# Moving the query, key and value loads of an attention core from GpSimd's DMA queue to SyncE's

## The chip, the cores and the metric

The kernel runs on one core of a Trainium2 chip. The metric is the time of one execution on the device in microseconds (us), the median over runs. The core has a tensor engine (PE, with its weight loads shown apart as PEld), VectorE (DVE), ScalarE (ACT), GpSimd (POOL) and SyncE (SP). SP computes nothing: it issues transfers (DMAs) on a queue of its own, in order, and each waits there for the buffers and data that it needs. GpSimd issues transfers too, between its own arithmetic, on a second queue. The profile calls the first queue q1, "hardware_dynamic", and GpSimd's q0, "software_dynamic". Both move their bytes with the same 16 DMA engines of the core.

## What is computed

The reference is a two-layer encoder trunk on 1024 tokens of 1024 features, all in float32: a retention layer, a squared-ReLU MLP, an attention layer, a second MLP and a last norm. The change touches the attention layer only. Cut to what matters:

```
q, k, v = split(h @ w_in, 3)              # 16 heads of 64 features
for each chunk c of 64 queries:           # 16 chunks
    keys  = the chunk itself and the 8 chunks before it
    s = q k^T * 64**-0.5 + bias[head][clipped distance]
    p = softmax(s);  o = p v
return o @ w_out
```

## The kernel before

Every float32 product is made from split operands: `hi` is the value rounded to the tensor engine's float32r, `lo` the rest, so a dense product is three matmuls (L162 to L164).

**Before the core.** `qk_proj(p)` (L712 to L733) computes queries and keys of a pair of heads with 96 such matmuls, splits them (`dhi` at L727, `t` at L729) and stores hi and lo in DRAM, in `qA[p]` and `kA[p]` (L733, eight stores for queries and eight for keys, on SP's queue). The buffers of `dhi` hold one tile for each half of the tokens, so the next split waits until the last one is stored. Values go to `vA` (L756). The order of work is p = 0 to 3, the values, then p = 4 to 7. The loads of heads 0 and 1 (L785 to L788) stand ahead of the last `qk_proj`, but each may run as soon as its data are in DRAM.

**The core.** It walks over 16 heads of four units each (`units`, L900). A unit is two blocks of 128 queries: `scores` (two products with the hi and the lo of the keys, L846 and L847; bias and minimum at L851; exponential at L855; scaling on GpSimd at L857), `turn` (transposes, L875, and a split) and `values` (L887, then sums and a split whose `lo` is GpSimd's, L141). Between them `fill.step` issues one group of the output product of earlier heads (`att_out`, from L162 to L164, `h` at L280), whose weights (`wraw`) come on SP's queue.

**The loads of a head** are asked for one head ahead, a step in each unit (`load_head`, L809 to L823):

- `load_q`: `qh`, 128 rows of 4 KB (64 hi rows and 64 lo rows). Two buffers.
- `load_k`: `kk`, 128 rows of 8 KB: 64 rows that hold keys' hi and lo, written twice, once for each half of the partitions. The source's pattern is `[[0, 2], [2 * S, DH], [1, 2 * S]]`: an outer step of two copies, then 64 rows, then 2048 words. 1 MB in all. Two buffers.
- `load_b`: `bt`, the bias, two transfers on SP's queue, and two small fills by GpSimd (L781, L782). Two buffers.
- the values: `vst`, 1024 pieces of 512 bytes. Three buffers.

A framework traces the program, lays every engine's instructions out in an order of its own that keeps the data's dependencies, and sets the waits. With two buffers, the keys of head n can be loaded once the last product of head n-2 that reads its keys (L847) is done.

Of the kernel before, what the change touches and what calls it, by code (L numbers as in the profile page):

```python
# [9 lines left out]
F32 = mybir.dt.float32  # L10
# [3 lines left out]
PSUM = bass.MemoryType.PSUM  # L14
DRAM = bass.MemoryType.DRAM

P = 128
# [9 lines left out]
DH = 64  # L27
# [15 lines left out]
def _tables():  # L43
    """Position tables: they depend on the shapes alone."""
    import numpy as np

    half = DK // 2
    inv = np.exp(-np.float32(np.log(10000.0)) * np.arange(half, dtype=np.float32) / np.float32(half))
    ang = (np.arange(S, dtype=np.float32)[:, None] * inv.astype(np.float32)[None, :]).astype(np.float64)
    cos = np.cos(ang).T.astype(np.float32)  # L50
    sin = np.sin(ang).T.astype(np.float32)
    lg = _log_gamma()
    jp = np.arange(S) % HT
    vdec = np.exp(-lg[None, :] * (jp[:, None] + 1.0)) * RET_SCALE
    vdec = vdec.reshape(NB, P, RH).transpose(1, 0, 2)
    ip = np.arange(HT)
    odec = np.exp(lg[None, :] * (ip[:, None] + 1.0)).reshape(HT // P, P, RH).transpose(1, 0, 2)
    j = np.arange(P)[:, None]
    i = np.arange(P)[None, :]
    same = (j // CHUNK) == (i // CHUNK)  # L60
    mask = np.zeros((P, RH, P))
    for h in range(RH):
        m = np.where(i >= j, 1.0, 0.0)
        mask[:, h, :] = np.where(same & (i < j), np.exp(2.0 * lg[h] * (j - i)), m)
    f = lambda a: np.ascontiguousarray(a, dtype=np.float32)
    return {
        "cos": f(cos),
        "sin": f(sin),
        "vdec": f(vdec),
        "odec": f(odec),  # L70
        "odec2": f(odec * odec),
        "mask": f(mask),
    }
# [3 lines left out]
def trunk_kernel(ctx: ExitStack, tc: tile.TileContext, I, out):  # L77
# [34 lines left out]
    def load_gains(psp, pl, parts, g0):  # L112
        """Gains of 128 features in a row each, turned so that the features lie on the partitions."""
        n = sum(src.shape[0] for src in parts)
        rows = pl.tile([n, P], F32, name="grows", tag=f"grows{g0}")
        r = 0
        for src in parts:
            DMA.dma_start(out=rows[r:r + src.shape[0], :], in_=src)
            r += src.shape[0]

        def turn():
            pg = psp.tile([P, n], F32, name="pg", tag="ps")
            nc.tensor.transpose(pg, rows, ident[0:n, 0:n])
            nc.vector.tensor_copy(out=gall[:, g0:g0 + n], in_=pg)
        return turn
# [8 lines left out]
    def split(src, hi, lo, hi_eng="act", lo_eng="dve"):  # L134
        """hi: src rounded to the tensor engine's float32r; lo: what is left of src, exactly."""
        if hi_eng == "act":
            nc.scalar.copy(out=hi, in_=src)  # L137
        else:
            nc.vector.tensor_copy(out=hi, in_=src)
        eng = nc.vector if lo_eng == "dve" else nc.gpsimd  # L140
        eng.tensor_tensor(out=lo, in0=src, in1=hi.bitcast(F32), op=ALU.subtract)  # L141

    def wload(src, kb, cols):
        """Fetch one weight unit [128, kb, cols] (1024 columns)."""
        raw = wp.tile([P, kb, cols], F32, name="wraw", tag="wraw", bufs=2)
        DMA.dma_start(out=raw, in_=src.rearrange("(k p) c -> p k c", p=P))
        return raw
# [11 lines left out]
    def mm3(ps, lhs, rhs, start, stop):  # L159
        """Three products that carry a float32 product of split operands."""  # L160
        (lh, ll), (rh, rl) = lhs, rhs
        nc.tensor.matmul(ps, lhsT=lh, rhs=rh, start=start, stop=False)  # L162
        nc.tensor.matmul(ps, lhsT=lh, rhs=rl, start=False, stop=False)  # L163
        nc.tensor.matmul(ps, lhsT=ll, rhs=rh, start=False, stop=stop)  # L164
# [4 lines left out]
    def rsqrt_newton(sd, v, y):  # L169
        """y = v ** -0.5, one Newton step past the square root's table."""  # L170
        nc.scalar.activation(sd, v, AF.Sqrt)
        nc.vector.reciprocal(out=y, in_=sd)
        nc.vector.scalar_tensor_tensor(out=sd, in0=v, scalar=-0.5, in1=y, op0=ALU.mult, op1=ALU.mult)
        nc.vector.tensor_tensor(out=sd, in0=sd, in1=y, op=ALU.mult)
        nc.vector.scalar_tensor_tensor(out=y, in0=sd, scalar=1.5, in1=y, op0=ALU.add, op1=ALU.mult)

# [1 line left out]
    class Norm:  # L178
# [28 lines left out]
        def finish(self, psp, hf, col=False, row=True):  # L207
            """r = rsqrt(mean + eps) of a half: along the free axis in rB, along the partitions in rcol."""
            ah = self.gp.tile([P, HT], F32R, name="ah", tag="ah")
# [18 lines left out]
    def up_group(psp, norm, w, hf):  # L228
        """128 output features of one half of the tokens."""
        hi, lo = w  # L230
        ps = psp.tile([P, HT], F32, name="ps", tag="ps")
        for kb in range(NB):
            mm3(ps, (hi[:, kb, :], lo[:, kb, :]), (norm.hi[kb][hf], norm.lo[kb][hf]), kb == 0, kb == NB - 1)
        return ps
# [5 lines left out]
    def proj_tok(psp, norm, src, evac):  # L240
        """512 output features, tokens on the partitions: one bank for each block of tokens."""
        pss = [psp.tile([P, HT], F32, name="ps", tag="ps") for _ in range(NB)]
# [10 lines left out]
    def down(box, src, nk, rhs, hi_eng="act", lo_eng="dve"):  # L253
        """h += W^T rhs for nk blocks of features, one group at a step. box holds the PSUM pool and, where
        the blocks are final, their norm; blocks that were final before the norm was there follow."""
        cols = 1024 // nk
# [35 lines left out]
    class Filler:  # L292
        """Steps of a product that are issued between other work."""

# [42 lines left out]

    # ================= retention =================
    vS = [dram.tile([S, DV], F32, name=f"vS{i}") for i in range(RH)]
# [137 lines left out]
    with ExitStack() as ph:  # L477
# [6 lines left out]
        with ExitStack() as st:  # L484
# [5 lines left out]

            # Loads run in the order of use, a ring of raw tiles ahead of the splits.
            items = [(hd, hf, what) for hd in range(RH) for hf in range(2) for what in ("q", "k", "v0", "v1")]
# [33 lines left out]
            def turn_k(hd):  # L526
                """Keys of the first half with the tokens on the partitions."""
                kt[hd] = th, tl = [cp.tile([P, 4, DK], F32R, name=n, tag=n, bufs=1) for n in ("kth", "ktl")]
# [45 lines left out]
            def outs(hd, hf, pr):  # L574
                """Retention of two blocks of queries and their normalised rows."""
                pss, mv = [], cp.tile([P, 2, 2], F32, name="mv", tag="mv", bufs=2)
# [115 lines left out]

    # ================= first MLP =================
    with ExitStack() as ph:
# [3 lines left out]

    # ================= chunked attention =================
    w_in = I["att_w_in"][0]  # L700
# [6 lines left out]
    with ExitStack() as ph:  # L707
# [57 lines left out]
        def load_q(hd):  # L765
            T[hd, "q"] = cq.tile([P, S], F32R, name="qh", tag="qh", bufs=2)
            nc.gpsimd.dma_start(out=T[hd, "q"], in_=qA[hd // 2][hd % 2].rearrange("z f c -> (z f) c"))

        def load_k(hd):
            t = cq.tile([P, 2, S], F32R, name="kk", tag="kk", bufs=2)  # L770
            src = kA[hd // 2][hd % 2]
            nc.gpsimd.dma_start(out=t.rearrange("p z s -> p (z s)"), in_=bass.AP(tensor=src.tensor, offset=src.offset, ap=[[0, 2], [2 * S, DH], [1, 2 * S]]))
            T[hd, "k"] = [t[:, 0, :], t[:, 1, :]]
# [18 lines left out]
    with ExitStack() as ph:  # L792
# [7 lines left out]
        with ExitStack() as st:  # L800
# [8 lines left out]
            def load_head(hd, step):  # L809
                """Stacks that give all four partial products of q k in two passes, values and bias."""  # L810
                if step == 0:
# [8 lines left out]
                else:  # L820
                    t = cp.tile([P, NB, P], F32R, name="vst", tag="vst", bufs=3)
                    nc.gpsimd.dma_start(out=t, in_=vA[hd // 8][:, (hd % 8) * P:(hd % 8 + 1) * P].rearrange("(t p) c -> p t c", p=P))
                    T[hd, "v"] = t  # L823
# [11 lines left out]
            def scores(hd, g, z):  # L835
                """Probabilities of one block of queries; scores and bias come negated."""
                Q = 2 * g + z
# [97 lines left out]

    # ================= second MLP and the last norm =================
    with ExitStack() as ph:
        psp = pool(ph, "psF", None, 8, PSUM)
        with ExitStack() as st:
# [4 lines left out]
            def last(src, rhs):  # L944
                """The last part of the product, half by half: one half leaves while the other is computed."""
                ws = []
# [63 lines left out]
```

## Time and profile before

| | us |
|---|---|
| median of 3 runs | 3043.75 (3042.92 to 3044.22) |
| span of the profiled execution, first to last instruction | 3039.2 |
| PE busy in the span | 2871.2 (94%) |
| DVE, ACT, POOL busy | 1319.7, 880.3, 432.5 |
| GpSimd's queue q0: packets, MB, share of 16 engines | 35584, 33.61, 5.1% |
| SP's queue q1 | 220896, 207.19, 22.4% |

The profiled execution's own time lies outside the profile; its span is 4.55 us under the median of the runs. Busy times of one engine can be read as shares of the span; the idle time that matters is that of PE, and nearly all of it lies in two places of the attention layer.

### The profile page before, as it was taken

The page shows a single profiled execution, that of the slowest core. Times are in us where ns is not written, and L with a number is a line of the kernel's source. Part 1 is how long each engine was busy: PE and PEld are TensorE (multiplying, and loading weights), DVE is VectorE, ACT ScalarE, POOL GpSimd, SP SyncE. Part 2 cuts the span into 40 slices and gives each one's busy share as a digit, 9 for nine tenths or more (in the row PEclk, how much of TensorE's full clock was granted, in tenths as well). Part 3 has the DMA queues.
Part 4 walks back from the last instruction along what each step waited for, and adds up shares of the span by engine and source line. Part 5 has one row for each costly group of instructions (what it writes and reads, how often), then busy time and mean ns, then how long its engine had stood idle before and what let it go on. Part 6 is the DMA issues. An engine that isn't in the chain of part 4 may idle for free.

```text
span 3039.2 us, 33109 instructions
## 1 busy us (share of the span) xinstructions
PE 2871.2 (94%) x13178; PEld 2376.4 (78%) x13178; DVE 1319.7 (43%) x2194; ACT 880.3 (29%) x1484; POOL 432.5 (14%) x439
## 2 busy tenths in 40 slices
PE   8999999899999999999999899576879999999998
PEld 7888888677778888888888788465767888888887
DVE  6331133555565333333346233465668333333335
ACT  4012222432342221112223122564655111222213
POOL 4320000322230000000002000454533000000002
PEclk9999999899999999999999999788989999999999
DMA  4323333432111111111114546645521111111111
GB/s 138 106 87 103 108 105 96 158 104 90 63 49 43 48 49 49 49 49 49 49 46 133 149 147 162 120 95 115 113 68 42 49 49 49 49 46 45 49 49 70
DMA packets 258122, 245.86 MB, mean 81 GB/s; under 512 B 25048, under 2 KB 209440, under 8 KB 255920
## 3 DMA queue, kind: packets, MB, share of 16 engines
q1 hardware_dynamic: 220896, 207.19, 22.4%
q0 software_dynamic: 35584, 33.61, 5.1%
q10 hardware_dynamic: 1488, 2.95, 0.3%
q8 instruction: 103, 1.69, 0.2%
q14 instruction: 51, 0.42, 0.0%
HBM read 189.09 MB, written 57.19 MB: 81 GB/s over the span
## 4 chain that ended last, share of the span: by engine, by line
PE 83%; DMA 10%; DVE 4%; POOL 1%; ACT 1%; issue 1%; SPq 0%; POOLq 0%; ACTq 0%; DVEq 0%
PE ps L162 26%; PE ps L163 26%; PE ps L164 26%; DMA kk<-kA 7%; PE po L887 1%; PE pt L875 1%; DVE hlo L190 0%; DMA kA<-dhi 0%; PE pS L846 0%; POOL acc L200 0%; DMA xt<-in_x_dram 0%; PE pS L847 0%; PE pt L629 0%; DMA wraw<-in_att_w_in_dram 0%; DMA qA<-dhi 0%
## 5 line engine op out<-in xcount | busy, mean ns | idle before, releaser
L162 PE MATMUL ps<-hhi,whi 128*128 128x512 f32 x1792 | 699.3, 390 | 12.5 <-ACT whi L137 9.3
L163 PE MATMUL ps<-hlo,whi 128*128 128x512 f32 x1792 | 698.8, 390 | 1.4 <-DVE hlo L190 1.4
L164 PE MATMUL ps<-hhi,wlo 128*128 128x512 f32 x1792 | 698.5, 390 | 1.0 <-DVE wlo L141 0.9
L137 ACT CAST whi<-wraw 128x1024 fp32r<-128x1024 f32 x220 | 231.6, 1053 | 1255.1 <-PE ps L163 1023.4
L280 DVE TENSOR_TENSOR h<-ps,h 128x512 f32<-128x512 f32 x368 | 253.6, 689 | 467.5 <-PE ps L164 465.4
L162 PEld LDWEIGHTS ps<-hhi,whi 128*128 128x128 f32 x1792 | 337.2, 188 | 83.6 <-ACT whi L137 10.0
L163 PEld LDWEIGHTS ps<-hlo,whi 128*128 128x128 f32 x1792 | 337.3, 188 | 72.1 <-DVE hlo L190 2.1
L164 PEld LDWEIGHTS ps<-hhi,wlo 128*128 128x128 f32 x1792 | 337.1, 188 | 72.2 <-DVE wlo L141 2.1
L162 PE MATMUL ps<-uh,whi 128*128 128x512 f32 x960 | 379.7, 396 | 0.0
L163 PE MATMUL ps<-ul,whi 128*128 128x512 f32 x960 | 379.7, 396 | 0.0
L164 PE MATMUL ps<-uh,wlo 128*128 128x512 f32 x960 | 379.7, 396 | 0.0
L141 DVE TENSOR_TENSOR wlo<-wraw,whi 128x1024 fp32r<-128x1024 f32 x213 | 266.7, 1252 | 239.4 <-ACT whi L137 239.3
L200 POOL TENSOR_TENSOR acc<-acc,sq 128x512 f32<-128x512 f32 x70 | 102.4, 1465 | 1418.0 <-ACT sq L199 1412.2
L324 DVE SCALAR_TENSOR_TENSOR t<-ps,rB 128x512 f32<-128x512 f32 x128 | 88.0, 691 | 320.6 <-PE ps L164 320.6
L162 PEld LDWEIGHTS ps<-uh,whi 128*128 128x128 f32 x960 | 180.3, 188 | 43.7
L164 PEld LDWEIGHTS ps<-uh,wlo 128*128 128x128 f32 x960 | 180.3, 188 | 43.6
L163 PEld LDWEIGHTS ps<-ul,whi 128*128 128x128 f32 x960 | 180.3, 188 | 43.6
L846 PE MATMUL pS<-kk,qh 128*128 128x320 f32 (+1 forms) x192 | 70.0, 370 | 107.2 <-DMA kk<-kA 102.4
L325 ACT ACTIVATE t<-t 128x512 f32<-128x512 f32 x128 | 80.5, 630 | 262.1 <-DVE t L324 262.1
L162 PE MATMUL ps<-whi,hhi 128*128 128x512 f32 x384 | 149.4, 389 | 0.3 <-DVE vt L755 0.3
L164 PE MATMUL ps<-whi,hlo 128*128 128x512 f32 x384 | 149.4, 389 | 0.0
L163 PE MATMUL ps<-wlo,hhi 128*128 128x512 f32 x384 | 149.4, 389 | 0.0
(188 smaller groups left out, 3760.3 us busy)
## 6 DMA issues: line engine op xcount, KB each, us to landing
wraw<-in_mlp_w_dram SPq DMA_DIRECT2D x128, 512.0 KB, 3.7
wraw<-in_ret_w_in_dram SPq DMA_DIRECT2D x48, 512.0 KB, 4.0
kk<-kA POOLq DMA_DIRECT2D x16, 1024.0 KB, 27.4
wraw<-in_att_w_in_dram SPq DMA_DIRECT2D x24, 512.0 KB, 3.9
vS<-t SPq DMA_DIRECT2D x32, 256.0 KB, 2.0
gS<-t SPq DMA_DIRECT2D x32, 256.0 KB, 2.1
wraw<-in_ret_w_out_dram SPq DMA_DIRECT2D x16, 512.0 KB, 3.5
raw<-vS SPq DMA_DIRECT2D x16, 512.0 KB, 4.5
```

The costliest lines, as they stand in the source:

```text
L137: nc.scalar.copy(out=hi, in_=src)
L141: eng.tensor_tensor(out=lo, in0=src, in1=hi.bitcast(F32), op=ALU.subtract)
L162: nc.tensor.matmul(ps, lhsT=lh, rhs=rh, start=start, stop=False)
L163: nc.tensor.matmul(ps, lhsT=lh, rhs=rl, start=False, stop=False)
L164: nc.tensor.matmul(ps, lhsT=ll, rhs=rh, start=False, stop=stop)
L200: nc.gpsimd.tensor_tensor(out=self.acc[hf], in0=self.acc[hf], in1=sq, op=ALU.add)
L280: nc.vector.tensor_tensor(out=hv, in0=ps, in1=hv, op=ALU.add)
L324: nc.vector.scalar_tensor_tensor(out=t, in0=res[hf], scalar=0.0, in1=rB[:, hf * HT:(hf + 1) * HT], op0=ALU.max, op1=ALU.mult)
L325: nc.scalar.activation(t, t, AF.Square)
L846: nc.tensor.matmul(ps[:, y, :hw], lhsT=qs, rhs=kh[:, ks], start=True, stop=False)
L875: nc.tensor.transpose(pt[:, c - done:c - done + P], pr[:, (kb - k0) * P:(kb - k0 + 1) * P], ident)
L887: nc.tensor.matmul(po[:, oc:oc + n], lhsT=T[hd, "v"][:, kb, :], rhs=t[:, off[kb]:off[kb] + n], start=i == 0, stop=i == len(seq) - 1)
```

## The change

The three loads of a head go to SP's queue (`DMA` is `nc.sync`), and their destinations are named as float32 in place of float32r, so that source and destination have one type. Source patterns, destinations, sizes and buffers stay as they are. The diff also empties docstrings and comment lines, which issue nothing and keep the line numbers.

```diff
         def load_q(hd):
             T[hd, "q"] = cq.tile([P, S], F32R, name="qh", tag="qh", bufs=2)
-            nc.gpsimd.dma_start(out=T[hd, "q"], in_=qA[hd // 2][hd % 2].rearrange("z f c -> (z f) c"))
+            DMA.dma_start(out=T[hd, "q"].bitcast(F32), in_=qA[hd // 2][hd % 2].rearrange("z f c -> (z f) c"))
 
         def load_k(hd):
             t = cq.tile([P, 2, S], F32R, name="kk", tag="kk", bufs=2)
             src = kA[hd // 2][hd % 2]
-            nc.gpsimd.dma_start(out=t.rearrange("p z s -> p (z s)"), in_=bass.AP(tensor=src.tensor, offset=src.offset, ap=[[0, 2], [2 * S, DH], [1, 2 * S]]))
+            DMA.dma_start(out=t.rearrange("p z s -> p (z s)").bitcast(F32), in_=bass.AP(tensor=src.tensor, offset=src.offset, ap=[[0, 2], [2 * S, DH], [1, 2 * S]]))
             T[hd, "k"] = [t[:, 0, :], t[:, 1, :]]
...
                     t = cp.tile([P, NB, P], F32R, name="vst", tag="vst", bufs=3)
-                    nc.gpsimd.dma_start(out=t, in_=vA[hd // 8][:, (hd % 8) * P:(hd % 8 + 1) * P].rearrange("(t p) c -> p t c", p=P))
+                    DMA.dma_start(out=t.bitcast(F32), in_=vA[hd // 8][:, (hd % 8) * P:(hd % 8 + 1) * P].rearrange("(t p) c -> p t c", p=P))
                     T[hd, "v"] = t
```

## Rows read from the trace of the kernel before

**Rows 1.** The page: the chain that ended last, and an issue's landing time.
```profile
PE 83%; DMA 10%; DVE 4%; POOL 1%; ACT 1%; issue 1%; SPq 0%; POOLq 0%; ACTq 0%; DVEq 0%
...
kk<-kA POOLq DMA_DIRECT2D x16, 1024.0 KB, 27.4
```

**Rows 2.** Waits of PE in 1895 to 2300: total us, times, longest.
```profile
PE pS L846 <- DMA kk<-kA: 102.4, 8, 15.5
PE pS L846 <- DVE sm L851: 4.6, 4, 3.6
```

**Rows 3.** PE's timeline in the core: start, us, instruction, idle before it.
```profile
1910.63 0.31 PE L847 MATMUL pS<-kk,qh 128*128 128x320 f32 x1
...
1924.91 0.31 PE L847 MATMUL pS<-kk,qh 128*128 128x320 f32 x1
...
1941.32 0.47 PE L846 MATMUL pS<-kk,qh 128*128 128x128 f32 x1 [15.48 <-DMA kk<-kA]
...
2067.40 0.45 PE L846 MATMUL pS<-kk,qh 128*128 128x128 f32 x1 [12.98 <-DMA kk<-kA]
...
2083.36 0.31 PE L847 MATMUL pS<-kk,qh 128*128 128x320 f32 x1
2085.76 0.22 PE L846 MATMUL pS<-kk,qh 128*128 128x128 f32 x1
...
2100.36 0.31 PE L847 MATMUL pS<-kk,qh 128*128 128x320 f32 x1
2115.77 0.45 PE L846 MATMUL pS<-kk,qh 128*128 128x128 f32 x1 [12.67 <-DMA kk<-kA]
```

**Rows 4.** The chain in order of time: start, us, what.
```profile
1971.89 0.45 PE pS L846
...
2085.68 29.96 DMA kk<-kA
...
2257.45 0.44 PE pS L846
```

**Rows 5.** Windows, core 0: length, busy times, PE's clock, DMA share, GB/s.
```profile
2083.00:2088.00 5.00, 4.98 (x36) 4.38 (x35) 4.67 (x14) 4.70 (x13) 3.53 (x5) 1.00 0.99 231
...
2094.00:2100.00 6.00, 6.00 (x41) 5.47 (x41) 4.97 (x16) 5.12 (x13) 4.79 (x5) 1.00 0.14 53
2101.00:2109.00 8.00, 1.91 (x9) 1.22 (x8) 3.01 (x9) 2.72 (x7) 5.17 (x8) 0.94 1.38 237
2110.00:2114.00 4.00, 0.00 (x0) 0.00 (x0) 0.00 (x0) 0.00 (x0) 0.00 (x0) 0.50 0.27 103
```

**Rows 6.** DMA by queue, 2094 to 2100: packets, MB, share of 16 engines.
```profile
q0 software_dynamic: 39, 0.32, 14.2%
```

**Rows 7.** Issues of 2101 to 2109: size, us from issue to landing.
```profile
kk<-kA POOLq DMA_DIRECT2D x1, 1024.0 KB, 25.1
vst<-vA POOLq DMA_DIRECT2D x1, 512.0 KB, 17.6
qh<-qA POOLq DMA_DIRECT2D x1, 512.0 KB, 16.4
bt<-skew SPq DMA_DIRECT2D x2, 144.0 KB, 12.8
```

**Rows 8.** Line L772 in the core: landing time of its 14 transfers, us.
```profile
DMA to landing us min/median/max: 24.4/27.2/30.3
```

**Rows 9.** GpSimd's timeline: the three issues of one head.
```profile
2100.09 0.98 POOL L822 DMA_DIRECT2D vst<-vA  x1
...
2102.58 0.62 POOL L767 DMA_DIRECT2D qh<-qA  x1
...
2104.03 0.86 POOL L772 DMA_DIRECT2D kk<-kA  x1
```

**Rows 10.** SP's timeline: weights ahead of the core and in it.
```profile
1860.64 0.59 SPq L146 DMA_DIRECT2D wraw<-in_att_w_in_dram  x1
...
1871.52 0.59 SPq L146 DMA_DIRECT2D wraw<-in_att_w_out_dram  x1
...
1905.95 0.53 SPq L146 DMA_DIRECT2D wraw<-in_att_w_out_dram  x1
```

**Rows 11.** Waits of all engines in 1660 to 1725: total us, times, longest.
```profile
ACT dhi L727 <- DMA kA<-dhi: 20.1, 4, 8.2
ACT dhi L727 <- DMA qA<-dhi: 9.0, 2, 6.7
...
PE ps L162 <- ACT whi L137: 8.0, 1, 8.0
POOL kk L772 <- DMA kA<-t: 7.0, 2, 6.3
```

## The prediction

> **What bounds the kernel now.** I read the page first. PE is the chain for 83% of the span, but a tenth of the chain is DMA, and of the issues that take longest to land one stands out: `kk`, the keys, with 27.4 us for 1 MB [rows 1]. The waits of PE over the attention core come next: PE stands still for 102.4 us there, in 8 waits, each time at the first product of a head, for `kk`; nothing else holds it for more than 5 us [rows 2]. So in the core the path runs through this one load.
>
> PE's timeline shows the rhythm. A head's first product starts at 2067.40 and its last at 2083.36; the next head starts at 2085.76, 18.4 us after the first, without a wait; the head after that would start some 17.3 us later, at 2103.1, but gets its keys at 2115.77 [rows 3]. Both key buffers are in turn: the load for the third head can be issued only when the first head is done (2083.67), GpSimd issues it at 2085.68, and it lands 29.96 us later [rows 4]. From the fourth head (1971.89) to the last (2257.45) that makes 285.6 us for 12 heads, 23.8 us each [rows 4], where the work alone takes about 17.3 to 18.4.
>
> Why does 1 MB take so long? The windows tell. While `kk` moves alone (2094 to 2100), the core's DMA moves 53 GB/s at a share of 0.14 [rows 5], and only GpSimd's queue has packets, 14.2% of 16 engines [rows 6]: 2.3 engines by busy time, so two engines with overlapping packets. One load alone therefore takes 1,048,576 B / 53 GB/s = 19.8 us. Just before, the same GpSimd queue fills the engines: 231 GB/s at 0.99 in 2083 to 2088 [rows 5], when `qh`, also GpSimd's, is on its way. So the narrowness belongs to this load, whose source is the only one with an outer step of two, and not to GpSimd's queue. Two `kk` together move 103 GB/s at 0.27 [rows 5]: on GpSimd's queue consecutive loads can take different pairs of engines.
>
> **The change part by part.**
>
> *The casts to 32-bit words.* The same bytes to the same places: no instruction more or less on PE, DVE and ACT. The source pattern of `kk` is kept with its outer step of two. I take it that it stays on two engines: 0 gained in width (the other end is a rival below).
>
> *GpSimd's issues go.* 48 issues of 0.62 to 0.98 us [rows 9], 16 x (0.98 + 0.62 + 0.86) = 39 us of GpSimd, 2.5 us a head. GpSimd waits for PE in each `kk` stall, so this hides behind the load: 0, and the 2.0 us from 2083.67 to 2085.68 if the load stood first. SP issues about 1 us after the last product, query first: 1 us of each stall saved, inside the terms below.
>
> *Queue order, the main term.* On GpSimd's queue a transfer behind a running `kk` already pays: the values and queries issued at 2100.09 and 2102.58 [rows 9] land after 17.6 and 16.4 us [rows 7], about when the running `kk` does (2115.77). They are wide, so each has a share on the two busy engines and waits for it. Now everything on SP's queue stands in that line: bias, weights, stores. And if SP's queue sends every `kk` to the same two engines, the keys of one head start only after those of the head before. No row shows which engines SP's queue picks. The ends are "the same two each time" and "pairs that change", as on GpSimd's. I take the first, as a choice: the changing pairs are seen only on the queue whose descriptors are software's.
>
> The Trainium skill, page "DMA: Bandwidth & Descriptors", section "Why a DMA increments its semaphore by 16 and not by 1", says that the engine count follows the slowest dimension of both patterns, on either kind of queue, and that a SyncE transfer gets the lowest-numbered engines while GpSimd's go round by a cursor. By that rule every `kk` would share engines 0 and 1, which is the sum below; by the changing pairs seen on GpSimd's queue it would be the first rival's.
>
> Then these two engines set the pace, per head: 19.8 us for `kk`; a sixteenth of queries, values and bias, (512 + 512 + 288) KB / 16 = 84 KB at 26.5 GB/s = 3.2 us; weights, 8 x 512 KB over 16 heads, 16 KB = 0.6 us. Together 23.6 us: the lower bound. `kk` also slows when others move: the two loads of 2101 to 2109 share 237 GB/s at a share over 1 [rows 5], and landing runs from 24.4 to 30.3 us, median 27.2 [rows 8]. The upper bound takes the median as the load's own time: 27.2 + 3.8 = 31.0. I take 26.1, nearer the low end: 2.5 us of slowing, since part of the 24.4 to 27.2 is lag ahead of the first byte and time in line, not transfer. The third head's keys are free to load at 1910.9 [rows 3], and land at about 1936 (1 us issue, 19.8 + 2.5 and 2 of lag) in place of 1941.32. From there 13 heads: 1936 + 13 x 26.1 = 2275, against 2257.45: **+18 us**. With 23.6 it is -14, with 31.0 it is +82.
>
> *The first two heads.* Their keys are loaded during the projections, where SP stores `dhi` and `t`. In this stretch ACT already waits 29.1 us for stores to land, and PE loses 8.0 [rows 11]. With both `kk` on SP's queue, the stores and weights issued behind stand in line for up to 2 x 19.8 = 39.6 us. Also SP now waits for key stores to land (GpSimd did, 7.0 us [rows 11]), with the next projection's stores and weights queued behind it. The next `dhi` can't be written until the last is stored, ACT stands, and no new weights are split. The cover is the two weight units already split, 10.9 us of PE each (SP's weight issues 1860.64 and 1871.52 [rows 10]): 39.6 - 21.8 = 17.8. **+18 us**, between 0 (loads spread out) and 40 (no cover).
>
> *Weights in the core*: the output product's are fetched far ahead (the fourth unit at 1905.95 [rows 10], before the first of them is used), so standing behind a `kk` costs 0; without that lead, up to one `kk` each. Bias and values come after the keys in line and are needed later: 0 beyond the 3.8 us counted.
>
> Sum: +18 + 18 = +36. The profiled span is 3039.2; what lies around it, to the median, is 4.55 us. 3039.2 + 36 + 4.55 = **3080 us**. By the bounds alone, 3044 - 14 + 0 = 3030 to 3044 + 82 + 40 = 3166.
>
> **Rivals.**
>
> *Two engines, but a different pair each time (faster).* Then SP's earlier issue is what is left: 2083.67 + 1, and a landing of about 25 us (low end of [rows 8]) give 2109.7, where 2115.77 stood: 6 us for each pair of heads. The fourth head's keys, whose buffer is free at 1925.2 [rows 3] but which land at 1971.89, would come at 1925.2 + 26 = 1951 or so. The last head starts at 1951 + 6 x (48.4 - 6) = 2205, 52 us earlier: **2992**. For it: two `kk` at 103 GB/s [rows 5]. It decides if consecutive loads overlap.
>
> *All 16 engines (faster).* 1 MB at the 231 GB/s of [rows 5] takes 4.5 us, inside the 17.3 us of the head between. The 102.4 us of waits [rows 2] go, and about 1 us after each of the eight, where the head runs 18.4 in place of 17.3: 3044 - 110 = **2933**. For it: `qh` and `vst` are wide. Against: the pattern of `kk` isn't changed.
>
> The same page of the Trainium skill, section "Issuing engine by pattern", has SyncE for simple loads and calls that path generally faster; it speaks for these two rivals, and gives no figure for this load.
>
> *In line, but hidden.* The pace is 23.8 as now, and the first loads lie apart: **3044**, within 6 us. For it: the lower bound of 23.6.
>
> **How the numbers follow.** In line on the same two engines, slower: 0.64. Different pairs: 0.14. All engines: 0.14. In line but hidden: 0.08. A measurement of this kernel tells 0.2%, 6 us, from no change. Faster: the two rivals, 0.28; same: 0.05 of the last; slower: 0.64 and the rest, 0.67. The forecast's own range is 3030 to 3145. The range 2975 to 3145 takes in the changing pairs, and leaves out all engines (0.14) and the far ends (0.06).
>
> **What would show it.** Right: a lone `kk` still at about 53 GB/s and a share of 0.14, never 100 with two in flight; PE's waits for `kk` at nearly every head, of 6 to 9 us, not at every other; `kk` landing over 30 us after its issue; stores and weights at 1660 to 1730 landing over 20 us late and PE idle there for some 25 us. Wrong: 100 GB/s and more while only keys move, key waits gone (all engines), or 103 GB/s at two in flight with the waits still in pairs (changing pairs). The start term falls if the framework puts the first two key loads elsewhere on SP.

## The result and the profile after

| | us |
|---|---|
| before, median of 4 runs beside it | 3043.34 |
| after, median of 4 runs | 3083.17 (3079.8 to 3084.25) |
| ratio, 95% interval | 1.0128 (1.0113 to 1.0142) |
| span of the profiled execution, before and after | 3039.2, 3081.4 |

The change makes the kernel 1.3% slower, by some 40 us. The total is close to the forecast, but it is not the forecast's sum: of its two terms one was too small and the other didn't come at all. That the total came out is in part luck.

The page after, first the chain that ended last and then the issues. The landing time of `kk` is missing there.

```profile
PE 81%; DMA 10%; DVE 4%; SPq 2%; ACT 1%; POOL 1%; issue 1%; POOLq 0%; ACTq 0%; DVEq 0%
...
kk<-kA SPq DMA_DIRECT2D x16, 1024.0 KB
...
wraw<-in_att_w_in_dram SPq DMA_DIRECT2D x24, 512.0 KB, 13.8
```

Beside [rows 1], PE's share of the chain has fallen by two points, and SP's own issues have entered it with 2%. The waits of PE from 1600 to 2340 (total us, times, longest) say where:

```profile
PE pS L846 <- DMA kk<-kA: 128.8, 14, 12.3
PE ps L162 <- DVE t L725: 6.0, 1, 6.0
PE pS L846 <- DVE sm L851: 4.4, 3, 3.6
```

Before there were 8 waits for `kk`, of 102.4 us together [rows 2]. Now each head from the third on waits, 14 of 14. PE's timeline shows the new rhythm: the core's start, the third, fourth, ninth and tenth head, and the last.

```profile
1899.49 0.22 PE L846 MATMUL pS<-kk,qh 128*128 128x128 f32 x1
...
1939.25 0.45 PE L846 MATMUL pS<-kk,qh 128*128 128x128 f32 x1 [12.26 <-DMA kk<-kA]
...
1965.97 0.45 PE L846 MATMUL pS<-kk,qh 128*128 128x128 f32 x1 [11.09 <-DMA kk<-kA]
...
2104.70 0.45 PE L846 MATMUL pS<-kk,qh 128*128 128x128 f32 x1 [9.49 <-DMA kk<-kA]
...
2132.65 0.44 PE L846 MATMUL pS<-kk,qh 128*128 128x128 f32 x1 [8.83 <-DMA kk<-kA]
...
2299.84 0.45 PE L846 MATMUL pS<-kk,qh 128*128 128x128 f32 x1 [5.74 <-DMA kk<-kA]
```

From the fourth head to the last that is (2299.84 - 1965.97) / 12 = 27.8 us a head, where it was 23.8 [rows 4], and the long and the short interval of [rows 3] have become one. The last head starts 42.4 us later than in [rows 4], as much as the whole span has grown. Before the core nothing is lost; the core of the kernel before started at the same time, in its timeline of PE:

```profile
1900.12 0.22 PE L846 MATMUL pS<-kk,qh 128*128 128x128 f32 x1
```

One head in the chain after, in order of time (start, us, what):

```profile
2095.22 6.04 SPq L767
2101.32 31.20 DMA kk<-kA
2132.65 0.44 PE pS L846
```

The keys issued at 2101.32 land at 2132.52 (2101.32 + 31.20). Those of the head before landed just ahead of 2104.70. So 27.8 of the 31.2 us lie between the landing of one head's keys and that of the next. What moves in that time, in the windows (length, busy times, PE's clock, DMA share, GB/s):

```profile
2060.00:2065.00 5.00, 5.00 (x36) 4.60 (x35) 4.03 (x12) 4.31 (x12) 4.12 (x4) 1.00 0.13 54
2109.50:2121.00 11.50, 11.50 (x78) 10.61 (x77) 9.13 (x23) 8.85 (x21) 6.20 (x8) 1.00 0.13 54
```

and by queue from 2109.5 to 2121 (packets, MB, share):

```profile
q1 hardware_dynamic: 74, 0.61, 12.7%
```

54 GB/s at a share of 0.13, about two of 16 engines, as in [rows 5, 6], but now from SP's queue. In no window above do keys move at the 103 GB/s that two loads made together on GpSimd's queue [rows 5].

### The profile page after: what moved, and what is told of

Read it like the earlier page. It is cut to its first block, busy times and chain, and to the rows that moved or that the text cites. A ratio compares the mean times of both kernels' runs of the same rounds, so it can differ in the third digit from the quotient of the medians.

```text
span 3081.4 us, 33131 instructions
## 1 busy us (share of the span) xinstructions
PE 2887.1 (94%) x13178; PEld 2391.3 (78%) x13178; DVE 1319.5 (43%) x2194; ACT 880.9 (29%) x1484; POOL 395.1 (13%) x391
## 4 chain that ended last, share of the span: by engine, by line
PE 81%; DMA 10%; DVE 4%; SPq 2%; ACT 1%; POOL 1%; issue 1%; POOLq 0%; ACTq 0%; DVEq 0%
PE ps L163 26%; PE ps L162 26%; PE ps L164 26%; DMA kk<-kA 8%; SPq L767 1%; PE po L887 1%; PE pt L875 1%; DMA wraw<-in_att_w_in_dram 1%; DVE hlo L190 0%; PE pS L846 0%; PE pS L847 0%; DMA xt<-in_x_dram 0%; POOL acc L200 0%; PE pt L629 0%; DMA raw<-vS 0%
## 5 line engine op out<-in xcount | busy, mean ns | idle before, releaser
L846 PE MATMUL pS<-kk,qh 128*128 128x320 f32 (+1 forms) x192 | 71.9, 380 | 133.3 <-DMA kk<-kA 128.8
L846 PEld LDWEIGHTS pS<-kk,qh 128*128 128x128 f32 x192 | 41.0, 214 | 141.6 <-issue 102.8
## 6 DMA issues: line engine op xcount, KB each, us to landing
wraw<-in_att_w_in_dram SPq DMA_DIRECT2D x24, 512.0 KB, 13.8
```

The costliest lines, as they stand in the source:

```text
L846: nc.tensor.matmul(ps[:, y, :hw], lhsT=qs, rhs=kh[:, ks], start=True, stop=False)
```

## The experiments

Theory A is the prediction's: on SP's queue each `kk` goes to the same two engines, so these two set the pace. Against it stand, as causes of the loss, the change of types, the queries and values, the issues and their order on SP, and the first two loads. Each is told apart below. The diffs are against the changed kernel unless another is named; times are medians, with the ratio to the kernel before and its 95% interval.

**The types alone**, as a change of the kernel before. GpSimd's queue keeps all three loads, whose destinations are named as float32.

```diff
-            nc.gpsimd.dma_start(out=T[hd, "q"], in_=...)
+            nc.gpsimd.dma_start(out=T[hd, "q"].bitcast(F32), in_=...)
...
```

> All three loads on GpSimd's queue as before, only their destinations named as 32-bit words, so that nothing is cast. Theory A: the cast is not the cost, 3043 us within 0.3%, a lone key load at 53 GB/s. Theory B (the cast slows the key packets): the key load moves at 60 GB/s or more and the time falls by 20 us or more.

3043.78, ratio 1.0005 (0.9995 to 1.0015): no change. A lone `kk` moves as in [rows 5], in the windows of this kernel:

```profile
2094.00:2100.00 6.00, 6.00 (x41) 5.42 (x40) 4.97 (x15) 5.13 (x12) 4.79 (x5) 1.00 0.13 53
```

The naming of the types costs and gives nothing that this run can tell; what is left of the change is the queue.

**The keys alone on SP.**

```diff
-            DMA.dma_start(out=T[hd, "q"].bitcast(F32), in_=...)
+            nc.gpsimd.dma_start(out=T[hd, "q"], in_=...)
...
-                    DMA.dma_start(out=t.bitcast(F32), in_=vA...)
+                    nc.gpsimd.dma_start(out=t, in_=vA...)
```

> Keys on SyncE's queue, queries and values back on GpSimd's. If every key load on SyncE's queue goes to the same two engines (theory A), keys still move one at a time: never much over 53 GB/s while only keys move, a key wait at nearly every head, but without the wide loads in line the pace falls from 27.8 us a head to 21.5 to 24: 3000 to 3045 us. If instead the pairs change and the wide loads or SyncE's long issues made the line (theory B), two key loads overlap at about 100 GB/s, the waits stay in pairs and the time falls to 2980 to 3000 us.

3069.54, ratio 1.0087 (1.0072 to 1.0102): slower than A gave. The waits of PE in the core, and a window in which a `kk` moves:

```profile
PE pS L846 <- DMA kk<-kA: 116.1, 14, 11.9
```

```profile
2075.00:2083.00 8.00, 8.00 (x47) 7.42 (x47) 5.05 (x15) 4.33 (x11) 2.18 (x4) 0.83 0.14 52
```

The mechanism holds (14 waits, 52 GB/s), and the size was missed. The chain has the fourth head at 1967.48 and the last at 2286.27, 26.6 us each. The expectation took queries and values on the other queue to leave the key engines alone; they cost almost as much there as from SP's own. In this order 26 of the 40 us come from the keys' move and 14 from putting the rest in the same queue. The split holds for this order alone: moved by themselves, queries and values gain 13 us, as the next run shows.

**The queries and values alone on SP.**

```diff
-            DMA.dma_start(out=t.rearrange("p z s -> p (z s)").bitcast(F32), in_=bass.AP(...))
+            nc.gpsimd.dma_start(out=t.rearrange("p z s -> p (z s)"), in_=bass.AP(...))
```

> Queries and values on SyncE's queue, keys back on GpSimd's. Theory A: the loss belongs to the keys alone, so it goes: keys overlap again at about 100 GB/s on changing pairs, and as GpSimd's queue holds nothing but keys they start earlier: 3000 to 3040 us, not above 3045. Theory B (the wide loads on SyncE's queue cost by themselves, through its issue order or its waits): 3055 us or more.

3030.37, ratio 0.9958 (0.9943 to 0.9973), with 94.8 us of waits for `kk` in 7 waits. A window with keys on their way:

```profile
2124.00:2128.00 4.00, 0.00 (x0) 0.00 (x0) 0.00 (x0) 0.00 (x0) 0.00 (x0) 0.50 0.27 100
```

This part of the change helps by 13 us: GpSimd's queue then holds the keys alone, and they still move two at a time, at 100 GB/s in this window. The loss comes with the keys' move.

**The keys in turn on two hardware queues.** SP has the odd heads, ScalarE's queue (q10) the even ones. If each queue had engines of its own, two loads would move at 103 GB/s.

```diff
-            DMA.dma_start(out=t...bitcast(F32), in_=bass.AP(...))
+            (DMA if hd % 2 else nc.scalar).dma_start(out=t...bitcast(F32), in_=bass.AP(...))
```

> As the changed kernel, but the keys of even heads are issued by ScalarE on its own queue, those of odd heads by SyncE. If both queues send these loads to the same two engines (theory A), two key loads in flight still move about 53 GB/s together, and the pace stays near 26 to 29 us a head: 3070 to 3110 us (ScalarE may also stand in its issues). If the line is only the order within SyncE's queue (theory B), two in flight move about 100 GB/s and the time falls below 3030 us.

3076.69 in one run. Two loads, issued on two queues (the timelines of ACT and of SP), are in flight together:

```profile
1972.22 0.50 ACTq L772 DMA_DIRECT2D kk<-kA  x1
```

```profile
1980.56 0.53 SPq L772 DMA_DIRECT2D kk<-kA  x1
```

The window 1996 to 2004, and the packets of both queues in it:

```profile
1996.00:2004.00 8.00, 0.00 (x0) 0.00 (x0) 0.00 (x0) 0.00 (x0) 0.00 (x0) 0.50 0.13 52
```

```profile
q1 hardware_dynamic: 26, 0.21, 6.4%
q10 hardware_dynamic: 25, 0.20, 6.2%
```

Both queues have packets, each at half of the share that one load had alone, and together they move 52 GB/s. Four engines at half their speed would give the same sum. The trace's packet records (start, length and queue of each) rule that out: in this window two packets are in flight for 98% of the time and never more than three, and packets of the two queues follow each other without a pause, 0.31 us each. In 2110 to 2114 of the kernel before, with two `kk` on GpSimd's queue [rows 5], four or more are in flight all the time. That shows A: the two engines are the same ones, not only for SP but for both hardware queues. The Trainium skill, "DMA: Bandwidth & Descriptors", section "Why a DMA increments its semaphore by 16 and not by 1", has the hardware queues use the lowest-numbered engines; this window agrees with it so far as both queues use the same two, whose numbers the trace doesn't give.

**The keys without wide loads.** Queries of heads 2 to 15 and values of heads 3 to 15 aren't loaded; older tiles take their place. Keys, bias and weights move as in the changed kernel.

```diff
         def load_q(hd):
+            if hd >= 2:
+                T[hd, "q"] = T[hd - 2, "q"]
+                return
...
+                elif hd >= 3:
+                    T[hd, "v"] = T[hd - 3, "v"]
```

> As the changed kernel, but the queries of heads 2 to 15 and the values of heads 3 to 15 are not loaded at all: those heads use the tiles of earlier heads, so the attention output is another one; every other instruction stays. Theory A (the two engines' own work sets the pace, of which the wide loads' shares and their slowing of the keys are the rest above 20 us): the pace falls from 27.8 to 21.5 to 23 us a head, and the time to 2995 to 3030 us. Theory B (SyncE's way of issuing, with its instructions of 8 to 9 us, or lag from one key load to the next sets the rest): 26 us a head or more, 3055 us or more.

3005.67, ratio 0.9873 (0.9853 to 0.9893). The fourth and the last head in PE's timeline, where the edit has moved the product of L846 to L851:

```profile
1958.58 0.48 PE L851 MATMUL pS<-kk,qh 128*128 128x128 f32 x1 [5.98 <-DMA kk<-kA]
...
2225.34 0.33 PE L851 MATMUL pS<-kk,qh 128*128 128x128 f32 x1 [2.02 <-DMA kk<-kA]
```

22.2 us a head, and PE still waits 14 times. Keys, bias and weights alone are slower than the 17.3 to 18.4 us of PE's work, as A says, and the queries and values add 27.8 - 22.2 = 5.6 us to each head.

**The first two key loads on GpSimd's queue**, the others on SP's.

```diff
-            DMA.dma_start(out=t...bitcast(F32), in_=bass.AP(...))
+            (DMA if hd >= 2 else nc.gpsimd).dma_start(out=t...bitcast(F32), in_=bass.AP(...))
```

> As the changed kernel, but the keys of heads 0 and 1 (loaded during the projections) stay on GpSimd's queue. By the prediction's term for the first two heads, 18 us of the loss are theirs: about 3065 us. By the trace of the changed kernel, in which the core starts at the same time as before, they cost nothing: 3083 us within 5.

3082.6, ratio 1.0124 (1.0107 to 1.0141), the same as the changed kernel. The prediction's second term is 0.

**The keys asked for before the queries.** In the head of the chain after that is shown above, SP's issue of `qh` (L767) takes 6 us ahead of the keys. If that set the pace, keys first would win it back.

```diff
-                if step == 0:
+                if step == 1:
                     if (hd, "q") not in T:
                         load_q(hd)
-                elif step == 1:
+                elif step == 0:
```

> As the changed kernel, but the keys of a head are asked for before its queries. Theory A (the two engines' own work sets the pace, and they are busy whatever the order): the pace stays at 27 to 28.5 us a head and the time within 8 us of 3083. Theory B (the query load, whose issue holds SyncE for 8 to 9 us, keeps the keys behind it out of the engines' line): keys follow each other closer, 25 us a head or less, 3045 us or less.

3076.52, ratio 1.0109 (1.0092 to 1.0126): 35 us lost beside its own kernel before, where the change lost 40, and the two intervals overlap. The waits of PE in the core have only changed their name:

```profile
PE pS L846 <- DMA qh<-qA: 127.1, 14, 12.8
```

The chain has the fourth head at 1968.77 and the last at 2296.91, 27.3 us each. So the order of the two isn't the cost. An issue that SP can't finish is still there in this kernel, now that of the keys (the last section), so this run alone doesn't show that such issues cost nothing. The packet records of the changed kernel do: from the fourth head to the last the keys' packets of 8 KB are missing for only 2.8% of the time, 0.8 us of each 27.8. One head's keys follow the other's almost without a gap, whatever SP's issues last.

**The keys in two transfers of 64 rows**, one for each half of the partitions, so that no pattern has the outer step of two.

```diff
-            DMA.dma_start(out=t.rearrange("p z s -> p (z s)").bitcast(F32), in_=bass.AP(..., ap=[[0, 2], [2 * S, DH], [1, 2 * S]]))
+            tw = t.rearrange("p z s -> p (z s)")
+            for z in range(2):
+                DMA.dma_start(out=tw[z * DH:(z + 1) * DH, :].bitcast(F32), in_=bass.AP(..., ap=[[2 * S, DH], [1, 2 * S]]))
```

> As the changed kernel, but the keys in two transfers of 64 rows, one for each half of the partitions, so that no source pattern begins with a step of two. Theory A (width): each half spreads over 16 engines, a head's keys land in under 10 us, PE's waits for keys (128.8 us) go to under 10, 2930 to 2955 us. Theory B (SyncE's queue or its long issues are the cost): still 3040 us or more.

2913.95 (2912.91 to 2914.81), ratio 0.9575 (0.9559 to 0.9591): 129 us faster than the kernel before and, with the next one, the fastest here. Its issues on the page (KB, median us to landing) and the waits of PE from 1600 on, where the lines stand two lower:

```profile
kk<-kA SPq DMA_DIRECT2D x32, 512.0 KB, 8.1
```

```profile
PE pS L848 <- DVE sm L853: 4.8, 4, 3.6
PE pt L877 <- DVE ptl L141: 3.2, 10, 0.8
```

No wait for keys is left. The gain is more than the 102.4 us of waits [rows 2]. The windows show a second part of it, first this kernel, then the core of the kernel before:

```profile
1900.00:2150.00 250.00, 242.94 (x1649) 219.34 (x1648) 215.70 (x615) 207.74 (x512) 139.47 (x216) 1.00 0.59 152
```

```profile
1900.10:2283.60 383.50, 272.35 (x1716) 245.88 (x1715) 229.00 (x641) 219.32 (x534) 180.17 (x267) 0.84 0.47 101
```

PE's granted clock is 1.00 throughout, where it was 0.84 over the core with its waits, and an instruction of PE takes 242.94 / 1649 = 0.147 us against 272.35 / 1716 = 0.159. For 1716 instructions of about the same mix that is an estimate of some 20 us on top of the waits. A third part lies ahead of the core, in this kernel's window and its first product:

```profile
1640.00:1740.00 100.00, 100.00 (x446) 82.94 (x445) 43.88 (x61) 20.19 (x28) 0.00 (x0) 1.00 0.70 186
```

```profile
1892.05 0.22 PE L848 MATMUL pS<-kk,qh 128*128 128x128 f32 x1
```

PE doesn't wait there, where it waited 8.0 us for `whi` before [rows 11], and the core starts 8.1 us earlier than at 1900.12. So narrow loads had held up the projections too, on GpSimd's queue already. PE was idle for 168 us in all before (3039.2 - 2871.2); the core's 111 and these 8 are 119 of them, most and not nearly all. The Trainium skill, "DMA: Bandwidth & Descriptors", section "Rules for kernel authors", warns of a leading broadcast of few copies, since it holds the whole transfer to that many engines. The two halves agree with it: 512 KB land after 8.1 us, where 1 MB with the broadcast needed 27.4 [rows 1].

**The same halves on GpSimd's queue**, as a change of the kernel before.

```diff
-            nc.gpsimd.dma_start(out=t.rearrange("p z s -> p (z s)"), in_=bass.AP(..., ap=[[0, 2], [2 * S, DH], [1, 2 * S]]))
+            tw = t.rearrange("p z s -> p (z s)")
+            for z in range(2):
+                nc.gpsimd.dma_start(out=tw[z * DH:(z + 1) * DH, :], in_=bass.AP(..., ap=[[2 * S, DH], [1, 2 * S]]))
```

> The kernel before (all three loads on GpSimd's queue, with casts), but the keys in the same two transfers of 64 rows. Theory A: the width is what counts, not the queue: 2935 to 2965 us, within 15 us of the same split on SyncE's queue. Theory B (GpSimd's queue is the slow one in the kernel before): 3010 us or more.

2915.1 (2912.24 to 2918.84), ratio 0.958 (0.9566 to 0.9594), and on its page:

```profile
kk<-kA POOLq DMA_DIRECT2D x32, 512.0 KB, 6.8
```

Once the load is wide, the queue makes no difference that these runs tell.

A third key buffer would show whether more loads ahead help while they are narrow. It wasn't tried.

## Why the prediction was right in its total

**The casts, GpSimd's issues and the width.** The casts cost 0, as the types alone showed. The two engines were right too: `kk` moves at 54 GB/s, in no window shown at 100. What GpSimd's missing issues are worth no run shows by itself.

**The same two engines.** This was a choice, with no row for it; the keys in turn on two queues show that it is so. The waits at every head came as told (14 of them), with 5.7 to 12.3 us in place of 6 to 9.

**The main term, mis-sized: +18 forecast, +42.4 measured.** The third head was put at 1936 and starts at 1939.25, 3 us of the miss. The rest is the pace, 26.1 forecast and 27.8 measured, over 13 heads. The kernel without wide loads splits it. Keys, bias and weights were worked out as 19.8 + 0.7 + 0.6 = 21.1 and took 22.2. Queries and values, their share of 2.5 and the slowing of 2.5, were put at 5.0 and took 5.6. Both parts were somewhat small, and thirteen heads multiply them. The range of 23.6 to 31.0 held it. The keys alone on SP show that most of the queries' and values' part isn't one of the queue: from GpSimd's queue they still left 26.6 us a head, 4.4 of the 5.6.

**The second term, failed: +18 forecast, 0 measured.** The step that failed is the stores and weights standing "in line for up to 2 x 19.8 = 39.6 us". SP's timeline after shows why:

```profile
1699.52 0.59 SPq L772 DMA_DIRECT2D kk<-kA  x1
...
1727.92 0.54 SPq L772 DMA_DIRECT2D kk<-kA  x1
```

The two loads are issued 28 us apart, and the 8 KB packets of the first end at 1723.2, so one is done before the other is asked for, and what stands behind has one load ahead of it. That is the lower bound of 0 which the prediction named ("loads spread out"). The stall did come, in the waits of all engines from 1640 to 1740:

```profile
ACT dhi L727 <- DMA qA<-dhi: 21.2, 2, 18.2
ACT dhi L727 <- DMA kA<-dhi: 3.8, 1, 3.8
```

ACT waited 18.2 us at once, where [rows 11] had waits of at most 8.2. The cover of 21.8 us that the prediction counted is more than that, and yet PE did wait, not for split weights but 6.0 us for `t` (L725, in the waits after), a wait that the prediction didn't count. PE's busy time in the two windows after:

```profile
1692.00:1704.00 12.00, 12.00 (x54) 9.95 (x53) 3.90 (x5) 2.23 (x3) 0.00 (x0) 1.00 0.76 191
1704.00:1730.00 26.00, 19.97 (x82) 16.08 (x81) 6.23 (x8) 3.80 (x5) 0.00 (x0) 0.87 0.38 119
```

PE lost 6.0 us in the second window, and before it lost 8.0 for `whi` [rows 11]. The new stall took the place of the old one, and the core starts at 1899.49, not later than before. The two halves, with which PE loses nothing here, show that the old one came from the narrow loads too: the kernel before had already paid for what this term forecast. The 25 us of idle PE that were to show this step don't exist.

**The sum.** +18 and +18 made the 36 that came out as some 40 by +42 and 0. The forecast of the total held since one term's miss covered the other's, which is luck; the mechanism of the main term is shown, that of the second was wrong for these loads.

**The rivals.** Pairs that change are excluded by the 52 GB/s of two loads in flight. All 16 engines would have been worth 110 us by the prediction, and the halves are worth 129. The price held the waits and 8 us for slower work after them; of the estimated 20 us of slower work it lacked 12, and it lacked the 8 us ahead of the core. The load in line but hidden falls with 27.8 us a head.

## What to carry to other kernels

Before moving a transfer to another queue, read from a window in which it moves alone how many engines it has; if the share is 0.13 and the core waits for it, its pattern is worth more than its queue (129 us here, against 40 lost). In these runs narrow loads on hardware queues share the same two engines, also from two queues, so a load that overlapped with its neighbour on GpSimd's queue stands in line on SP's. Where a term depends on when two transfers are issued, price it for both places in the order: here the two loads came 28 us apart, and the forecast 18 us were 0. And look whether the kernel before already pays for the same stall.

## What the runs showed that was not expected

SP's issue itself gets long while a narrow load of its own queue is on its way. SP's timeline after:

```profile
2092.98 8.29 SPq L767 DMA_DIRECT2D qh<-qA  x1
2101.32 0.54 SPq L772 DMA_DIRECT2D kk<-kA  x1
2101.94 3.94 SPq L779 DMA_DIRECT2D bt<-skew  x2
```

The `qh` issue takes 8.29 us, though the load before it needed 0.36 (`vst` at 2089.48); GpSimd's issue of the same load took 0.62 [rows 9]. With the keys on GpSimd's queue SP's issue of `qh` has a median of 0.34 us, so it isn't the narrow load alone, but one on the same queue. Weights for the projections land after 13.8 us on the page after. With the keys first it is the key issue that lasts 8.32 us, and the pace moves only from 27.8 to 27.3. Why the issue is held isn't shown; that it doesn't set the pace follows from the keys' packets, which leave 0.8 us a head free.

Wide loads slow a narrow one from any queue: 22.2 us a head without queries and values, 26.6 with them on GpSimd's queue, 27.8 on SP's. And the wait costs twice, since PE's clock falls with it: the granted clock is 0.50 while PE waits (1996 to 2004 with the keys in turn), 1.2 in place of 2.4 GHz, and the first product after a wait takes 0.45 us where the one at 1899.49, with no wait ahead of it, takes 0.22.
